# The convolution's output projection by seven products for each two feature tiles, with layer 1's memory values made in layer 0

## The chip, the core and the metric

The kernel runs on one core of a Trainium2 chip. The metric is the device time of one execution in microseconds (us). A core has five engines that work side by side, each through a list of instructions of its own: TensorE (PE; its weight loads are shown apart as PEld), VectorE (DVE), ScalarE (ACT), GpSimd (POOL) and SyncE (SP). In this kernel SP issues all transfers between DRAM and the on-chip memory SBUF. TensorE writes its results into banks of a second memory, PSUM, which VectorE and ScalarE read.

## The reference

A trunk of two layers over 1024 tokens with 1024 features, in float32. Layer 0 is windowed attention beside a retention, layer 1 a gated short convolution, and behind each stands a cross-attention into 256 memory tokens:

```
def conv_mixer(xn, w_in, conv_w, conv_b, w_out):
    gb, gc, u, gate = jnp.split(xn @ w_in, 4, axis=-1)
    z = gc * u
    ...                                 # conv = causal convolution of z over 3 tokens
    y = gb * conv * jax.nn.silu(gate)
    return y @ w_out

def memory_cross_attention(xn, memn, wq, wkv, wo):
    q = xn @ wq
    k, v = jnp.split(memn @ wkv, 2, axis=-1)
    ...
    return softmax(q k^T / 16) v @ wo   # 4 heads of 256

for i in range(2):
    x = x + (even_mixer if i == 0 else conv_mixer)(rmsnorm(x, ...), ...)
    x = x + memory_cross_attention(rmsnorm(x, c_norm[i]), rmsnorm(mem, c_mem_norm[i]), ...)
return rmsnorm(x, final_norm)
```

Rewritten here is `y @ w_out` in layer 1; moved is the half `v` of `memn @ wkv` of layer 1.

## The kernel before

x is kept transposed, as eight tiles of 128 features by 1024 tokens. Each float32 product is made as three products of split halves: a value is its rounded half (hi) plus the rest (lo), and `mm3` (L189, L190, L191) multiplies hi by hi, lo by hi and hi by lo. A split is a cast on ScalarE (L205) and a subtraction on VectorE (L206); for a weight tile L87 and L88, or L106 and L107 where only a page of 512 columns is made. A dense output tile of 128x512 is 8 x 3 = 24 products of 512 columns.

The stages, by their place in the span: layer 0's mixer (0 to about 455 us), its output projection with the memory values of layer 0 (to 545), the cross-attention (to 693), the output projection of that (`out_proj_halves`, to 815: eight output tiles for the first token half, beside which `keys_out` makes layer 1's memory keys and stores them in DRAM, then eight for the second), the convolution's input projection (`conv_in`, to about 1133), its output projection (`out_proj`, to 1240), the second cross-attention (to 1380) and the last projection.

`conv_in` already makes two output tiles at a time by seven products in place of eight, the Strassen-Winograd scheme on 2x2 blocks: `right_factors` makes from the normalized x the blocks B11, B21, B22 and the differences T1 to T4, each of four tiles of 512 columns, split; the class `Weights` makes from two weight tiles the factors A11, A12, A22 and the sums S1 to S4 (S1 to S4 on POOL at L99 to L102, or on VectorE); `strassen` runs the products, each 4 x 3 = 12 of 512 columns, and copies a finished product out of PSUM where a second one needs it (`kept`, L642). `times` multiplies the outputs into z and y (on POOL at L683, for one half of each).

`out_proj` before makes the eight output tiles densely, 16 x 24 = 384 products. For each it loads the old residual tile (`xold`, L287), adds it when the result leaves PSUM (L291), squares the result over `xold` (ACT, L247), adds that to the sum of squares `ssq` (POOL, L249) and stores the new tile (L297). Between them `mem_v` makes the memory values, 96 products, from memory tiles that layer 1 loads again. Behind it `norm` makes R, the reciprocal root of the mean square: two products with a matrix of ones for each token half (L256, L257), then ACT and VectorE (L228 to L233); products of the next stage (q, banks `psd`) run under it and are scaled by R as they leave PSUM (L278).

What sets the order: every tile is one of a few rotating buffers of its tag, so its first write waits for the last reader of the buffer's former tile. The context orders each engine's list by a simulated timeline and gives the listed order; `issue_after` binds one instruction behind another. Weights stream in the order of one list (`order`), two raw tiles at a time (WRAW), three split ones ahead (WHI, WLO). The buffers by tag:

```
BUFS = {"xh": 8, "xl": 8, "r": 8, "e": 4, "T": 5, "v": 4, "t": 5, "k": 4, "n": 2}
```

`v` holds the `xold` tiles; the PSUM banks are three of tag `d`, two `sc` and three `a`.

Of the kernel before, what the change touches and what calls it, by code (L numbers as in the profile page):

```python
# [22 lines left out]
P = 128  # L23
# [8 lines left out]
EARLY = 4  # L32
# [8 lines left out]
class Weights:  # L41
# [5 lines left out]
    FACTORS = ("A11", "A12", "S1", "S2", "S3", "S4", "A22")  # L47
    LATER = FACTORS[2:]

    def __init__(self, tc, pool, sums, order):  # L50
# [10 lines left out]
        for _, f in self.units:  # L61
            self.tags.append(("whi", "wlo") if f is None else (("whi", "wlo")[pages % 2],))
            pages += f is not None
# [4 lines left out]
    def load(self, i):  # L68
# [4 lines left out]
        for k, ap in enumerate(entry[:2] if isinstance(entry, tuple) else (entry,)):  # L73
            t = self.pool.tile([P, D], F32, tag="wraw", bufs=WRAW, name=f"wraw{i}_{k}")
            for c in halves(i == 0):
                self.nc.sync.dma_start(t[:, c], ap[:, c])
# [15 lines left out]
    def factor(self, u, i, f):  # L92
        if f == self.order[i][2][0]:
# [9 lines left out]
            self.factors = F  # L103
        t = self.page(self.tags[u][0], f"wf{u}")
        src, hi, lo = self.factors[f], t[:, :H], t[:, H:]
# [3 lines left out]
        if f == self.order[i][2][-1]:  # L109
            self.raw.pop(i)  # L110

    def prepare(self, upto=None):

        while self.next < len(self.units) and (upto is None or self.next <= upto):
# [6 lines left out]
            if f is None:  # L121
                self.whole(u, i)
            else:
                self.factor(u, i, f)
# [11 lines left out]
class Trunk:  # L136
# [144 lines left out]
    def out_proj(self, ys, x_old, x_new, between=iter(())):  # L281
# [17 lines left out]
        return xs, old  # L299

# [263 lines left out]
    def right_factors(self, x, gain, h, out):  # L564
# [6 lines left out]
             for i in range(2) for j in range(2)}  # L571
        def normed(f):
            for k in range(4):
# [4 lines left out]
        def split(f, src):  # L578
            for k in range(4):
                if f in ("T2", "T1"):  # L580
# [3 lines left out]
                else:  # L584
                    tag = {"B11": "xh", "B21": "xh", "T3": "xl", "B22": "xl", "T4": "Tn"[k // 2]}[f]
                    t = self.buf(tag, f, dt=F32R)
# [12 lines left out]
        T2 = [t[:, i, :] for t in (self.buf("T", "T2", (P, 2, H)) for _ in range(2)) for i in range(2)]  # L599
# [23 lines left out]
        with ExitStack() as behind:  # L623
            for make in (t1, t2, t3, lambda: split("B22", B["B22"]), t4):
                last = make()
                behind.enter_context(self.tc.issue_after(last.ins))
                behind.enter_context(self.tc.issue_after(self.last_cast.ins))

    def strassen(self, B, out, early=False):
# [3 lines left out]
        def product(ps, f, first, weights=None):  # L633
            ah, al = weights or self.w.take()
            with self.tc.issue_after(self.last_mm.ins) if early == 0 and early is not False else ExitStack():
# [4 lines left out]
        def kept(ps):  # L640
            t = self.buf("t", "kept", (P, H))
            self.nc.scalar.copy(t, ps)  # L642
            return t

        a, b = self.ps("sc" if early is False or early < 2 else "d"), self.ps("d")
        if early is False:
            product(a, "B11", True)
            p1 = kept(a)
            product(b, "B21", True)
# [428 lines left out]
```

## Time and profile before

| | us |
|---|---|
| median of 3 runs | 1484.68 (1483.44 to 1486.18) |
| the profiled execution | 1482.23 |
| its span in the profile | 1480.1 |
| span of the rewritten stage, about | 1134 to 1240 |

The span is the time from the first to the last instruction that the profile shows; 2.1 us of the execution lie around it. A page of the profile lists for each engine the busy time, the share of the span and the number of instructions. A row of groups names line, engine, operation, output <- inputs with shapes and the count, then total busy us, mean ns, and what ended the idle time before them. A row of the timeline gives start, length, engine, line and operation, and in brackets the idle time of that engine before it and what ended that. In a table by stretch, the first numbers are the stretch and its length, then busy us (and instructions) of PE, PEld, DVE, ACT and POOL, then TensorE's granted clock as a share of full speed, the DMA engines' busy share and GB/s.

### The profile page before, as it was taken

The numbers are of one execution on the slowest core, as the hardware profiler recorded it, in microseconds if no ns is written. First come the engines' busy times: TensorE is split into PE (matmuls) and PEld (weight loads), VectorE is DVE, ScalarE is ACT, GpSimd is POOL, SyncE is SP. The second block draws the span as 40 slices with busy tenths as digits, with TensorE's granted clock in tenths as the row PEclk, the third lists the DMA queues.
The fourth block names the chain that finished last, engine by engine and source line by source line (L and its number), as shares of the span: only waits on it lengthen the run. The fifth ranks groups of instructions, "written<-read, shape, count | busy, mean of one in ns | idle before, by whom it ended". The sixth has DMA issues, their size and how long they took to land.

```text
span 1480.1 us, 18711 instructions
## 1 busy us (share of the span) xinstructions
PE 1438.2 (97%) x7218; PEld 1215.4 (82%) x7218; DVE 878.1 (59%) x1289; ACT 634.8 (43%) x1139; POOL 322.7 (22%) x201
## 2 busy tenths in 40 slices
PE   8999999999899999999999799999999999999996
PEld 6888888888788888888888578888888888888996
DVE  7656765656674346446456967666665337446555
ACT  6434662334463344335344533333352325335554
POOL 2300103233311110000213455333340220000233
PEclk9999999999999999999999899999999999999999
DMA  6410114221365421013764121111125532111364
GB/s 216 149 65 29 58 30 142 61 79 48 119 224 170 151 92 43 29 42 129 226 201 143 42 86 58 57 57 57 58 86 213 186 128 72 39 33 40 127 210 152
DMA packets 51625, 153.38 MB, mean 104 GB/s; under 512 B 6352, under 2 KB 14672, under 8 KB 51024
## 3 DMA queue, kind: packets, MB, share of 16 engines
q1 hardware_dynamic: 51536, 152.19, 31.7%
q8 instruction: 57, 0.93, 0.3%
q14 instruction: 32, 0.26, 0.1%
HBM read 122.80 MB, written 25.17 MB: 100 GB/s over the span
## 4 chain that ended last, share of the span: by engine, by line
PE 79%; DVE 8%; DMA 5%; POOL 3%; issue 2%; ACT 2%; SPq 0%; DVEq 0%; POOLq 0%; ACTq 0%
PE psd L191 17%; PE psd L189 17%; PE psd L190 17%; PE pssc L191 5%; PE pssc L189 5%; PE pssc L190 5%; PE psa L190 4%; PE psa L189 4%; PE psa L191 4%; DMA swap<-bk 1%; PE pssc L367 1%; DMA swap<-bq 1%; PE psa L397 1%; PE psa L871 1%; POOL bk L432 1%
## 5 line engine op out<-in xcount | busy, mean ns | idle before, releaser
L189 PE MATMUL psd<-xh,whi 128*128 128x512 f32 (+2 forms) x1096 | 414.2, 381 | 7.7 <-ACT whi L87 7.3
L190 PE MATMUL psd<-xl,whi 128*128 128x512 f32 (+2 forms) x1096 | 414.7, 379 | 0.0
L191 PE MATMUL psd<-xh,wlo 128*128 128x512 f32 (+2 forms) x1096 | 414.3, 379 | 0.2 <-DVE wlo L88 0.2
L189 PEld LDWEIGHTS psd<-xh,whi 128*128 128x128 f32 x1096 | 206.4, 188 | 43.2 <-ACT whi L87 7.8
L191 PEld LDWEIGHTS psd<-xh,wlo 128*128 128x128 f32 x1096 | 206.3, 188 | 35.6 <-DVE wlo L88 0.7
L190 PEld LDWEIGHTS psd<-xl,whi 128*128 128x128 f32 x1096 | 206.5, 188 | 34.0
L87 ACT CAST whi<-wraw 128x1024 fp32r<-128x1024 f32 (+1 forms) x135 | 140.8, 1045 | 213.9 <-PE psd L190 131.0
L88 DVE TENSOR_TENSOR wlo<-wraw,whi 128x1024 fp32r<-128x1024 f32 (+1 forms) x135 | 169.1, 1254 | 71.1 <-ACT whi L87 71.0
L249 POOL TENSOR_TENSOR ssq<-ssq,xold 128x512 f32<-128x512 f32 (+2 forms) x54 | 84.6, 1567 | 574.5 <-ACT xold L247 503.0
L106 ACT CAST wf<-ws 128x512 fp32r<-128x512 f32 x64 | 39.7, 622 | 95.2 <-PE pssc L191 27.7
L291 DVE TENSOR_TENSOR xnew<-psd,xold 128x512 f32<-128x512 f32 x32 | 21.9, 690 | 96.4 <-PE psd L191 93.1
L189 PE MATMUL pssc<-T,wf 128*128 128x512 f32 x168 | 67.1, 399 | 6.6 <-ACT T L205 4.2
L190 PE MATMUL pssc<-T,wf 128*128 128x512 f32 x168 | 67.2, 400 | 1.9 <-DVE T L206 1.9
L191 PE MATMUL pssc<-T,wf 128*128 128x512 f32 x168 | 66.9, 398 | 0.0
L247 ACT ACTIVATE xold<-xnew 128x512 f32<-128x512 f32 (+2 forms) x63 | 36.5, 580 | 66.9 <-DVE xnew L291 37.1
L107 DVE TENSOR_TENSOR wf<-ws,wf 128x512 fp32r<-128x512 f32 x64 | 51.8, 811 | 20.7 <-ACT wf L106 19.6
L107 DVE TENSOR_TENSOR wf<-wraw,wf 128x512 fp32r<-128x512 f32 x40 | 55.1, 1393 | 5.0 <-ACT wf L106 5.0
L205 ACT CAST Th<-psa 128x512 fp32r<-128x512 f32 (+1 forms) x62 | 34.3, 588 | 54.2 <-PE psa L871 29.5
L206 DVE TENSOR_TENSOR Tl<-psa,Th 128x512 fp32r<-128x512 f32 (+1 forms) x62 | 41.7, 686 | 21.4 <-ACT Th L205 21.1
L278 DVE TENSOR_TENSOR q<-psd,R 128x512 f32<-128x512 f32 x32 | 22.1, 691 | 53.8 <-PE psd L191 53.8
L99 POOL TENSOR_TENSOR ws<-wraw 128x512 f32<-128x512 f32 x15 | 32.0, 2131 | 90.5 <-DMA wraw<-w_o_in 90.5
L189 PE MATMUL psd<-y,whi 128*128 128x512 f32 x128 | 50.0, 391 | 0.0
(324 smaller groups left out, 2949.4 us busy)
## 6 DMA issues: line engine op xcount, KB each, us to landing
wraw<-w_o SPq DMA_DIRECT2D x40, 512.0 KB, 4.2
wraw<-w_o_in SPq DMA_DIRECT2D x36, 512.0 KB, 3.6
wraw<-w_e_in SPq DMA_DIRECT2D x25, 512.0 KB, 3.6
wraw<-w_k SPq DMA_DIRECT2D x16, 512.0 KB, 3.9
xold<-x SPq DMA_DIRECT2D x16, 512.0 KB, 5.1
wraw<-w_v SPq DMA_DIRECT2D x16, 512.0 KB, 3.8
x<-xnew SPq DMA_DIRECT2D x16, 512.0 KB, 2.6
wraw<-w_q SPq DMA_DIRECT2D x16, 512.0 KB, 3.5
```

The lines of the kernel that those rows point to most:

```text
L87: self.nc.scalar.copy(hi[:, c], raw[:, c])
L88: self.nc.vector.tensor_tensor(lo[:, c], raw[:, c], hi[:, c].bitcast(F32), op=ALU.subtract)
L99: tt(F["S1"], F["A21"], F["A22"], op=ALU.add)
L106: self.nc.scalar.copy(hi, src)
L107: self.nc.vector.tensor_tensor(lo, src, hi.bitcast(F32), op=ALU.subtract)
L189: mm(o, ah, bh, start=first, stop=False, skip_group_check=more)
L190: mm(o, ah, bl, start=False, stop=False, skip_group_check=more)
L191: self.last_mm = mm(o, al, bh, start=False, stop=last, skip_group_check=more)
L205: self.last_cast = self.nc.scalar.copy(hi, src)
L206: return (eng or self.nc.vector).tensor_tensor(lo, src, hi.bitcast(F32), op=ALU.subtract)
L247: nc.scalar.activation(sq, x, AF.Square)
L249: eng.tensor_tensor(self.ssq[:, a:b], self.ssq[:, a:b], sq, op=ALU.add)
```

## The change

In words:

- `out_proj` of layer 1 becomes `out_proj_pairs`: four pairs of output tiles by seven products of 12, so 4 x 84 = 336 products instead of 384. The right factors are made from y (`right_factors` with no gain): B11 and T1 split into buffers of `xh`, T3 and B22 of `xl`, B21 and T2 of `e`, T4 two tiles of `T` and two of `v`; the four tiles of T2 before its split use two more of `v`.
- The residual: a pair's two `xold` tiles are loaded (L323) when the pair first keeps a product; the keep itself adds the residual (VectorE, L330, in place of a copy on ScalarE). When a result leaves PSUM the kept tile is added (L341, L343), the result is squared over `xold` and summed on POOL (L257).
- `OUT_EARLY = 2`: the B11 product of pairs 0 and 1 is run ahead, with its weights (512 columns) paged on their own; its keep is a copy, and the residual is added later.
- The memory values of layer 1 are made beside the keys in layer 0 (`values_out`), split, stored in DRAM and loaded again by `values_in`. The weights `w_v1` move there in the list; the second load of the memory tiles is gone.
- In `conv_in` the product of T4 comes before that of B22 (the factors' order changes with it), B22 is split last, and the multiplication of a half output by `second` goes from POOL to VectorE (L763).

The core of the diff:

```diff
-EARLY = 4
+EARLY, OUT_EARLY = 4, 2
...
+    def out_proj_pairs(self, B, x_old, x_new, early):
+        nc = self.nc
+        half = (slice(0, H), slice(H, S))
+        xs, rest, seen = [None] * KT, {}, set()
+        def pair(n):
+            old, new = [], []
+            def fetch():
+                for i in range(2):
+                    old.append(self.buf("v", "xold"))
+                    nc.sync.dma_start(old[i], x_old[2 * n + i])
+                new.extend(self.buf("r", "xnew") for _ in range(2))
+                xs[2 * n : 2 * n + 2] = new
+            def keep(i, j, ps):
+                t = self.buf("t", "kept", (P, H))
+                if i == j == 0 and n < early:
+                    nc.scalar.copy(t, ps)
+                    return t
+                if not old:
+                    fetch()
+                nc.vector.tensor_tensor(t, ps, old[i][:, half[j]], op=ALU.add)
+                return t
+            def out(i, j, ps, more):
+                c = half[j]
+                x, sq = new[i][:, c], old[i][:, c]
+                if i == j == 0 and n < early:
+                    nc.vector.tensor_tensor(sq, sq, more, op=ALU.add)
+                    more = None
+                nc.vector.tensor_tensor(x, ps, sq if more is None else more, op=ALU.add)
+                end = 2 * n + 2 == KT and i != j
+                self.squares(j in seen, x, sq, c.start, c.stop, None if end else nc.gpsimd)
+                seen.add(j)
+                if end:
+                    rest[j] = sq
+                nc.sync.dma_start(x_new[2 * n + i][:, c], x)
+            return self.strassen(B, out, keep, None, n < early)
...
-            for make in (t1, t2, t3, lambda: split("B22", B["B22"]), t4):
+            for make in (t1, t2, t3, t4, lambda: split("B22", B["B22"])):
...
         product(a, "T2", False)
-        u2 = kept(a)
+        u2 = keep(0, 1, a)
         product(a, "T3", False)
         out(1, 1, a, p5)
+        product(a, "T4", False)
+        out(1, 0, a, None)
         product(c, "B22", False)
         out(0, 1, c, u2)
-        product(a, "T4", False)
-        out(1, 0, a, None)
...
-                    nc.gpsimd.tensor_tensor(c, c, kept[0], op=ALU.mult)
+                    nc.vector.tensor_tensor(c, c, kept[0], op=ALU.mult)
...
-        self.out_proj_halves(ys, xd[0], xd[1], self.keys_out(self.mem_parts(1, "T")), after)
+        mem = self.mem_parts(1, "T")
+        both = (None for _ in zip(self.keys_out(mem), self.values_out(mem)))
+        self.out_proj_halves(ys, xd[0], xd[1], both, after)
         ys = self.conv_in(B)
         self.new_norm()
-        mem = self.mem_parts(1, "T")
-        K = self.keys_in()
-        kv = self.mem_v(mem)
-        V = next(kv)
-        ys = [self.split_k(y) for y in ys]
-        x, rest = self.out_proj(ys, xd[1], xd[2], kv)
+        B = {}
+        for h in range(2):
+            self.right_factors(ys, None, h, B)
+        x, rest = self.out_proj_pairs(B, xd[1], xd[2], OUT_EARLY)
+        K, V = self.keys_in(), self.values_in()
```

Where the lists change. Names are those of the program with a running number; `wraw` is a raw weight tile, `ws` a weight sum, `psd`, `pssc` and `psa` PSUM tiles, `x2` behind a row two of the same. POOL's list before, in the output projection, one row a residual tile:

```order
L249 TENSOR_TENSOR ssq_1058_9171<-ssq_1058_9171,xold_1089_9320 128x512 x2
L249 TENSOR_TENSOR ssq_1058_9171<-ssq_1058_9171,xold_1093_9426 128x512 x2
L249 TENSOR_TENSOR ssq_1058_9171<-ssq_1058_9171,xold_1099_9530 128x512 x2
L249 TENSOR_TENSOR ssq_1058_9171<-ssq_1058_9171,xold_1103_9636 128x512 x2
L249 TENSOR_TENSOR ssq_1058_9171<-ssq_1058_9171,xold_1107_9702 128x512 x2
L249 TENSOR_TENSOR ssq_1058_9171<-ssq_1058_9171,xold_1111_9768 128x512 x2
```

POOL's list now, from the middle of the stage on (9642 and 9644 are the residual tiles of pair 1, 9767 and 9769 of pair 2, 9913 and 9915 of pair 3):

```order
L102 TENSOR_TENSOR ws_1132_9797<-wraw115_1_9780 128x512
L104 TENSOR_TENSOR ws_1132_9797<-wraw115_0_9778,wraw115_1_9780 128x512
L257 TENSOR_TENSOR ssq_1072_9359<-ssq_1072_9359,xold_1115_9642 128x512
L103 TENSOR_TENSOR ws_1133_9798<-ws_1132_9797,wraw115_0_9778 128x512
L257 TENSOR_TENSOR ssq_1072_9359<-ssq_1072_9359,xold_1116_9644 128x512
L105 TENSOR_TENSOR ws_1133_9798<-wraw115_0_9778,ws_1133_9798 128x512
L257 TENSOR_TENSOR ssq_1072_9359<-ssq_1072_9359,xold_1125_9767 128x512
L257 TENSOR_TENSOR ssq_1072_9359<-ssq_1072_9359,xold_1126_9769 128x512
L257 TENSOR_TENSOR ssq_1072_9359<-ssq_1072_9359,xold_1125_9767 128x512
L257 TENSOR_TENSOR ssq_1072_9359<-ssq_1072_9359,xold_1126_9769 128x512
L257 TENSOR_TENSOR ssq_1072_9359<-ssq_1072_9359,xold_1137_9913 128x512
L257 TENSOR_TENSOR ssq_1072_9359<-ssq_1072_9359,xold_1138_9915 128x512
```

Between the sums of squares stand the sums for the weight factors, and each residual tile comes back twice with other work between.

SP's list before, as the third and the fourth residual tile are issued:

```order
L287 DMA xold_1093_9426<-x1_2_200 128x1024
L76 DMA wraw107_0_9305<-w_v1 128x1024
L287 DMA xold_1099_9530<-x1_3_201 128x1024
L76 DMA wraw108_0_9327<-w_o_out 128x1024
L297 DMA x2_0_206<-xnew_1084_9220 128x1024
L287 DMA xold_1103_9636<-x1_4_202 128x1024
```

SP's list now, from pair 2's residual tiles (9767, 9769) to those of pair 3 (9913, 9915):

```order
L323 DMA xold_1125_9767<-x1_4_202 128x1024
L323 DMA xold_1126_9769<-x1_5_203 128x1024
L79 DMA wraw116_0_9924<-w_q1 128x1024
L349 DMA x2_4_210<-xnew_1127_9771 128x512
L912 DMA K_1145_10029<-kd_6023 128x2048
L912 DMA K_1146_10030<-kd_6023 128x2048
L349 DMA x2_4_210<-xnew_1127_9771 128x512
L79 DMA wraw117_0_9961<-w_q1 128x1024
L349 DMA x2_5_211<-xnew_1128_9772 128x512
L323 DMA xold_1137_9913<-x1_6_204 128x1024
L349 DMA x2_5_211<-xnew_1128_9772 128x512
L79 DMA wraw118_0_9997<-w_q1 128x1024
L323 DMA xold_1138_9915<-x1_7_205 128x1024
```

Pair 3's loads stand behind stores of pair 2's results and between loads of the next stage's weights and of the keys.

TensorE's list at the border of pairs 2 and 3 now, from the end of pair 2's T4 (pssc 9750) to the start of pair 3's T2 (pssc 9896); before, dense tiles followed each other without a product that waits for a residual:

```order
L197 MATMUL pssc_1123_9750<-T4_1094_9443,wf217_9751 128x512
L198 MATMUL pssc_1123_9750<-T4_1094_9443,wf217_9751 128x512
L199 MATMUL pssc_1123_9750<-T4_1094_9443,wf217_9751 128x512
L197 MATMUL psd_1175_10107<-xh_1149_10037,whi226_9957 128x512
L197 MATMUL psd_1176_10133<-xh_1149_10037,whi226_9957 128x512
L197 MATMUL pssc_1135_9896<-T2_1085_9404,wf222_9858 128x512
```

Two products of the next stage (`psd` from `xh`) stand between, and T2 adds onto a bank whose former content must have been kept.

TensorE's list at the norm before, around the second product of the first token half (L257):

```order
L191 MATMUL psd_1145_9968<-xh_1127_9914,wlo206_9772 128x512
L189 MATMUL psd_1145_9968<-xh_1129_9918,whi206_9771 128x512
L257 MATMUL psa_1136_9932<-sq2_1135_9931,mean_dr_77 128x512
L190 MATMUL psd_1146_9994<-xl_1128_9915,whi206_9771 128x512
L191 MATMUL psd_1146_9994<-xh_1127_9914,wlo206_9772 128x512
L189 MATMUL psd_1146_9994<-xh_1129_9918,whi206_9771 128x512
L191 MATMUL psd_1147_10026<-xh_1125_9910,wlo207_9838 128x512
```

and at the norm now (psa 10071 and 10086 are the two token halves):

```order
L264 MATMUL psa_1166_10071<-sq2_1165_10070,mean_dr_77 128x512
L264 MATMUL psa_1170_10086<-sq2_1169_10085,mean_dr_77 128x512
L198 MATMUL psd_1175_10107<-xl_1164_10066,whi226_9957 128x512
L199 MATMUL psd_1175_10107<-xh_1163_10065,wlo226_9958 128x512
L198 MATMUL psd_1176_10133<-xl_1164_10066,whi226_9957 128x512
L199 MATMUL psd_1176_10133<-xh_1163_10065,wlo226_9958 128x512
L198 MATMUL psd_1177_10165<-xl_1164_10066,whi227_9993 128x512
L199 MATMUL psd_1177_10165<-xh_1163_10065,wlo227_9994 128x512
L265 MATMUL psa_1166_10071<-sq2_1165_10070,mean_dr_77 128x512
L265 MATMUL psa_1170_10086<-sq2_1169_10085,mean_dr_77 128x512
L197 MATMUL psd_1178_10191<-xh_1149_10037,whi227_9993 128x512
```

The two halves' statistics have moved together, with six q products between their first and their second product, and the fourth tile of q (psd 10191), for which one of the three `d` banks must come free, follows directly; before, that tile came 35 rows behind the first half's last product.

More of the change, by code (lines that the diff above doesn't have):

```diff
@@ L60, in __init__ @@
         pages = 0
-        for _, f in self.units:
-            self.tags.append(("whi", "wlo") if f is None else (("whi", "wlo")[pages % 2],))
-            pages += f is not None
+        for i, f in self.units:
+            paged = f is not None or order[i].shape[-1] < D
+            self.tags.append((("whi", "wlo")[pages % 2],) if paged else ("whi", "wlo"))
+            pages += paged
         self.next = 0
@@ L74, in load @@
             t = self.pool.tile([P, D], F32, tag="wraw", bufs=WRAW, name=f"wraw{i}_{k}")
[L75 removed]
+            t = t[:, : ap.shape[-1]]
+            for c in halves(True) if i == 0 else (slice(0, ap.shape[-1]),):
                 self.nc.sync.dma_start(t[:, c], ap[:, c])
@@ L103, in factor, with paged @@
             self.factors = F
+        self.paged(u, self.factors[f])
+        if f == self.order[i][2][-1]:
+            self.raw.pop(i)
+    def paged(self, u, src):
         t = self.page(self.tags[u][0], f"wf{u}")
-        src, hi, lo = self.factors[f], t[:, :H], t[:, H:]
+        hi, lo = t[:, :H], t[:, H:]
         self.nc.scalar.copy(hi, src)
@@ L120, in prepare @@
             self.load(i)
-            if f is None:
+            if f is None and len(self.tags[u]) == 1:
+                self.paged(u, self.raw.pop(i)[0])
+            elif f is None:
                 self.whole(u, i)
@@ L299, in out_proj @@
         return xs, old
+    def out_proj_pairs(self, B, x_old, x_new, early):
[33 more added lines that the diff above has]
+            return self.strassen(B, out, keep, None, n < early)
+        started = []
+        for n in range(early):
+            started.append(pair(n))
+            next(started[n])
+        for n in range(KT // 2):
+            for _ in started[n] if n < early else pair(n):
+                pass
+        return xs, rest
     def out_proj_halves(self, ys, x_old, x_new, between, after):
@@ L638, in product @@
                     self.mm3(ps, ah[:, c], al[:, c], bh, bl, first and k == 0, k == 3, not first)
[L640 to L646, printed above, removed]
+        a = self.ps("sc" if early is None or early < 2 else "d")
+        if early is None:
             product(a, "B11", True)
-            p1 = kept(a)
-            product(b, "B21", True)
+            p1 = keep(0, 0, a)
+            if apart:
+                yield
         else:
@@ L674, in times, with keep @@
         kept = []
+        def keep(i, j, ps):
+            t = self.buf("t", "kept", (P, H))
+            nc.scalar.copy(t, ps)
+            return t
         def out(i, j, ps, more):
@@ L689, in out @@
                 nc.vector.tensor_tensor(c, ps, c, op=ALU.mult)
-        return self.strassen(B, out, early)
+        return self.strassen(B, out, keep, early)
     def conv_start(self, B):
```

87 lines of the change are left out of this document (64 added, 23 removed).

## The prediction

> **What bounds the kernel now.** I read the page first, then a table by stage, then the waits of TensorE, then the timeline at the places that the change touches.
>
> ```profile
> span 1480.1 us, 18711 instructions
> PE 1438.2 (97%) x7218; PEld 1215.4 (82%) x7218; DVE 878.1 (59%) x1289; ACT 634.8 (43%) x1139; POOL 322.7 (22%) x201
> ```
>
> TensorE is busy for 97% of the span, so a product that goes saves its whole time, and a wait put in costs its whole length. The table by stage has, for each stretch, its length, the busy time of PE, PEld, DVE, ACT and POOL, the granted clock, the DMA share and GB/s. First the first half of layer 0's out projection, then the start of the convolution, then the stage that is rewritten:
>
> ```profile
> 705.00:764.00 59.00, 59.00 (x339) 52.10 (x338) 26.66 (x33) 21.91 (x31) 10.25 (x6) 1.00 0.74 231
> 815.00:860.00 45.00, 36.02 (x135) 27.12 (x133) 39.88 (x61) 22.09 (x38) 21.88 (x7) 0.89 0.17 54
> 1134.00:1240.00 106.00, 105.77 (x467) 87.11 (x466) 47.42 (x51) 40.17 (x48) 18.46 (x12) 1.00 0.43 149
> ```
>
> The rewritten stage has no slack to win: 0.23 us idle in 106. The place in this kernel where a stage of seven products starts already, 815 to 860, has 9.0 us of idle time and a clock of 0.89. The waits of TensorE say the same, for 1130 to 1300 and then (the largest two) for 680 to 900:
>
> ```profile
> PE psd L191 <- DVE wlo L88: 0.2, 1, 0.2
> ...
> PE pssc L189 <- ACT T L205: 4.2, 1, 4.2
> PE pssc L189 <- ACT kept L642: 2.4, 1, 2.4
> ```
>
> The question is thus whether 336 products can be fed as densely as the 384 were. One product's time, and the chain behind a finished tile:
>
> ```profile
> 1179.18 0.39 PE L189 MATMUL psd<-xh,whi 128*128 128x512 f32 x1
> ...
> 1183.71 0.39 PE L191 MATMUL psd<-xh,wlo 128*128 128x512 f32 x1
> ...
> 1184.14 0.69 DVE L291 TENSOR_TENSOR xnew<-psd,xold 128x512 f32<-128x512 f32 x1 [4.30 <-PE psd L191]
> ...
> 1184.91 0.62 ACT L247 ACTIVATE xold<-xnew 128x512 f32<-128x512 f32 x1
> ...
> 1185.68 1.74 POOL L249 TENSOR_TENSOR ssq<-ssq,xold 128x512 f32<-128x512 f32 x1 [3.76 <-ACT xold L247]
> ...
> 1187.44 0.33 SPq L287 DMA_DIRECT2D xold<-x  x1
> ```
>
> From the first to the second row are 20 starts in 4.53 us: 0.2265 us each. The last product of a tile starts at 1183.71; the residual is added, squared (over the old residual tile) and summed on POOL from 1185.68, 1.97 us after that product. Right at the end of the sum (1187.42) SP issues the next residual load: the load waited for the slot.
>
> **The change, part by part.**
>
> *48 products fewer:* 48 x 0.2265 = 10.9 us gained. The 96 value products only move to layer 0.
>
> *Convolution start.* The copy of the kept product stood behind four casts on ACT:
>
> ```profile
> 837.79 0.62 PE L191 MATMUL pssc<-T,wf 128*128 128x512 f32 x1
> 838.08 2.17 ACT L205 CAST B<-xnew 128x512 fp32r<-128x512 f32 x4
> ...
> 840.16 0.57 ACT L642 COPY kept<-pssc 128x512 f32<-128x512 f32 x1
> 840.78 0.50 PE L189 MATMUL pssc<-T,wf 128*128 128x512 f32 x1 [2.38 <-ACT kept L642]
> ```
>
> With B22's split last the copy follows the product's end (837.79 + 0.62) at once: about 1.5 us gained. T4 before B22 in the later pairs only reorders the same products. The multiplication of y and `second` goes from POOL to VectorE, which is 59% busy; next to the end of the stage it shortens the chain. Taken together 0 to 2, counted at 1.5.
>
> *The residual tiles.* The two T4 tiles hold two of the four `v` slots throughout the new stage, so a pair's residual tiles can be loaded only when the pair before has squared and summed its own in the same slots; before, four tiles rotated and a load ran about three tiles ahead. Now the load has a consumer at once: keeping a product adds the residual, and T2 and B22 wait for it. The prices: the POOL sum, the landing of the load in this stretch and, in the next line, over all its issues:
>
> ```profile
> L249 POOL TENSOR_TENSOR ssq<-ssq,xold 128x512 f32<-128x512 f32 x12 | 18.5, 1538 | 78.9 <-ACT xold L247 43.4 <-issue 30.7 <-DMA x<-xnew 4.8
> ...
> DMA to landing us min/median/max: 4.3/4.5/4.5
> DMA to landing us min/median/max: 3.1/5.1/6.8
> ```
>
> Pair 3: its first tile takes the slot of pair 2's first. From the last T3 product of pair 2 it is 1.97 to POOL, then the sums of T3 and B22 in a row (2 x 1.54), 4.4 landing and 0.8 for VectorE's add: 10.3 us. Meanwhile TensorE has T4's 12 products, two q products and one more, 15, 3.4 us, and then T2 of pair 3: 6.9 idle. Pair 2: on POOL two sums of the factors of weights S1 and S2 stand between the sums of pair 1 (the last row below has 1.38 us for one): from T3's last product of pair 1 1.97 + 1.54 + 1.38 + 1.38 + 1.54 + 4.4 + 0.8 = 13.0 us against about 39 products, 8.85: 4.15 idle. Pair 1, which is begun early, needs 1.97 + 1.54 + 4.4 + 0.8 = 8.7 against 35 products, 7.9: 0.85. T4 following T3 on the same bank: 0.5 once. Sum 12.4 us. Its ends: with landings of 3.1 and no S sums ahead on POOL about 8, with 6.8 and 1.74 per sum about 17. On SP the weight loads of later pairs stand behind the waiting residual loads; they have a pair's time, and I price them at nothing.
>
> ```profile
> L101 POOL TENSOR_TENSOR ws<-wraw,wraw 128x512 f32<-128x512 f32 x15 | 20.8, 1384 | 0.0
> ```
>
> *The norm behind it.* Before, the statistics' last product is followed by many q products; now q needs the buffers of T3 and B22, which come free with pair 3, so only six q products stand between the two halves' statistics, and the next q product needs a bank that only R can empty. R's chain:
>
> ```profile
> 1242.19 0.39 PE L257 MATMUL psa<-sq,mean_dr 128*128 128x512 f32 x1
> ...
> 1242.62 0.69 ACT L228 ACTIVATE rs<-psa,eps 128x512 f32<-128x512 f32 x1 [0.44 <-PE psa L257]
> ...
> 1244.01 0.63 ACT L230 ACTIVATE rt<-rs 128x512 f32<-128x512 f32 x1
> ...
> 1244.67 0.69 DVE L231 SCALAR_TENSOR_TENSOR rt<-psa,rt 128x512 f32<-128x512 f32 x1 [1.35 <-ACT rt L230]
> ...
> 1245.86 0.69 DVE L233 TENSOR_TENSOR R<-rt,rs 128x512 f32<-128x512 f32 x1
> ...
> 1248.28 0.69 DVE L278 TENSOR_TENSOR q<-psd,R 128x512 f32<-128x512 f32 x1 [1.73 <-PE psd L191]
> ```
>
> R is there 4.36 us after the product; emptying the bank takes 0.69, and between stands a step of the second half's chain, about another 0.7: 5.8 in all, less two products, 0.45: 5.35 idle. Lower end 3 (the halves do not interleave), upper 6.5.
>
> *The clock after a wait.* The row of 4.18 us idle at the convolution's start, and what follows it:
>
> ```profile
> 831.00 0.50 PE L189 MATMUL pssc<-T,wf 128*128 128x512 f32 x1 [4.18 <-ACT T L205]
> ...
> 834.38 0.63 PE L189 MATMUL pssc<-T,wf 128*128 128x512 f32 x1
> ...
> 835.00:838.00 3.00, 3.00 (x9) 2.11 (x7) 3.00 (x6) 2.25 (x4) 3.00 (x1) 0.50 0.00 0
> ```
>
> From 834.38 to 837.79 eight steps take 0.426 us each, at a granted clock of 0.50: about ten slow steps, 2 us, behind one long wait. Two of the new waits are longer than 4.18 (pair 3 and the norm), pair 2's is near: 3.5, from 2 to 7. The Trainium skill, "TensorE: Matmul & The Clock Gate", Part 1, The HAM clock gate, says that about one window (3.4 us) of idling halves the rate until about as long a busy stretch has passed. This trace agrees (0.50, 0.426 against 0.2265); by an estimate from that page alone each long wait would lose 1.7 us.
>
> *The way into the stage.* Before, a y tile's whole split was hidden. Now 28 half splits on ACT and VectorE and 16 subtractions on VectorE stand there, with the weights' sums on POOL, and T2, T3 and T4 need the last y tile. No row shows it for this stage. The low end is the stage as it was (nothing), the high end the convolution's own start, 9.0 us of idle and slow time beyond it, 12. The work is the same as there, but without gains and with the B11 and T1 products of pairs 0 and 1 as cover: 6, nearer to the second.
>
> *Layer 0.* The value products stand beside the keys. In 705 to 764 seven residual loads are issued, so a tile of the first half takes 59 / 7 = 8.4 us. The rows of that stretch's loads, and the cast and the subtraction of a weight tile:
>
> ```profile
> wraw<-w_o SPq DMA_DIRECT2D x10, 512.0 KB, 4.7
> ...
> xold<-x SPq DMA_DIRECT2D x7, 256.0 KB, 3.8
> ...
> L87 ACT CAST whi<-wraw 128x1024 fp32r<-128x1024 f32 (+1 forms) x135 | 140.8, 1045 | 213.9 <-PE psd L190 131.0
> L88 DVE TENSOR_TENSOR wlo<-wraw,whi 128x1024 fp32r<-128x1024 f32 (+1 forms) x135 | 169.1, 1254 | 71.1 <-ACT whi L87 71.0
> ```
>
> With 12 value products it takes 8.4 + 2.7 = 11.1 us and moves 2.62 MB (three weight tiles, keys, values, residual in and out), 235 GB/s; the row at 705 shows 231 GB/s without a wait. Three raw weight tiles go through two slots: 4.7 landing, 1.05 cast, 1.25 subtraction and 0.33 issue are 7.3, so 3.65 us a tile where 3.7 are to be had. That just fits; I take 2, from 0 to 10. Layer 1's stage loses the second load of the memory (four of 512 KB) and gains two loads of the values of 1 MB, off the path.
>
> Sum: -10.9 - 1.5 + 12.4 + 5.35 + 3.5 + 6 + 2 = +16.9 us. The profiled execution took 1482.23 us (span 1480.1), 0.17% under the median of 1484.68 (1483.44 to 1486.18). On the one base that gives 1499.1, on the other 1501.6; I say 1500.
>
> **The rivals.**
>
> *The residual arrives in time.* If a pair's load is issued before the wait counts (some 5.2 us ahead: 4.4 landing and 0.8), the 12.4 us and with them most of the clock loss fall away; norm 5.35 and a way in of 3 to 6 stay: 1484.68 - 12.4 + 5.35 + 3.5 = 1481, from 1476 to 1486. For it: POOL is only 22% busy, and before the load ran ahead. Against it: the slots, which only the sums release. It decides on the other side.
>
> *POOL shut out by VectorE.* A sum of two weight halves at the convolution's start:
>
> ```profile
> 834.20 13.49 POOL L99 TENSOR_TENSOR ws<-wraw 128x512 f32<-128x512 f32 x1 [34.67 <-DMA wraw<-w_o_in]
> ...
> 846.47 0.68 DVE L686 TENSOR_TENSOR second<-pssc,kept 128x512 f32<-128x512 f32 x1
> ```
>
> It took 13.49 us and ended just after VectorE, which had run operations with two SBUF inputs back to back, came to one that reads PSUM. The L101 row's 1.38 is what such a sum takes alone, so a shut-out costs 12.1. The new way in has 44 such VectorE operations (28 + 16) of some 0.6 us and needs POOL's S1 for T1 and S2 for T2; with the 36 products of B11 and T1 as cover (8.2 us), one shut-out leaves 4, two leave 16. This would put the way in at about 14 instead of 6: 1508, from 1503 to 1514. The Trainium skill, "SBUF — State Buffer", Who interferes with whom, states that such a VectorE instruction and a GpSimd one exclude each other for the whole instruction; this trace agrees in the 13.49 us, and what it would make of the time is this rival.
>
> *Layer 0 bound by its transfers.* If landings there grow from 4.7 to 5.5, a raw tile needs 4.05 us instead of 3.7, 24 tiles, 8.4 us: with 2 of it counted already, 1506. For it: 3.65 against 3.7; against it: three pages of split weights lie ahead.
>
> **How the numbers follow.** About 0.2%, 3 us, is what a measurement of this kernel can tell from no change. My forecast, 1500 (1491 to 1505, the ends of the smaller terms), has a chance of 0.50. The residual in time 0.23: 0.16 of it faster by over 0.2%, 0.07 within. POOL shut out 0.18, layer 0 bound 0.09, both slower. Slower 0.77, same 0.07, faster 0.16. The range 1481 to 1511 leaves out half of the first rival and the ends of the others.
>
> **What would show it.** In the profile after: TensorE with some 48 products fewer and a busy share that falls below 97%; waits of the T2 and B22 products of pairs 2 and 3 on the kept products, which sit behind the residual load on VectorE; POOL sums right ahead of SP's residual issues; a wait of about 5 us of the q product on R, with the granted clock under 0.9 behind both; idle time between 1100 and 1150. I am wrong if the kept products of pairs 2 and 3 wait for nothing, or if a q product fills the norm. Then the 10.9 us show in full. If layer 0 is the matter, waits on the split weights stand between 700 and 790.

## The result and the profile after

The changed kernel takes 1506.20 us (median of 4, 1505.49 to 1507.78) against 1484.47 for the kernel before: 1.0147 times as long, 95% interval 1.0129 to 1.0164. (1484.47 is the median of four runs; that of the three named ahead is 1484.68.) The profiled execution took 1505.49 us, its span 1503.4. The page, span and first section:

```profile
span 1503.4 us, 18770 instructions
...
PE 1440.5 (96%) x7170; PEld 1212.1 (81%) x7170; DVE 911.9 (61%) x1373; ACT 652.8 (43%) x1181; POOL 309.4 (21%) x201
```

TensorE has its 48 instructions fewer (7218 to 7170), but is busy for 2.3 us more, and the span has grown by 23.3. Fewer products with more busy time are slower products. The table by stretch (as before: length, then busy us of PE, PEld, DVE, ACT and POOL, the granted clock, the DMA share, GB/s) shows where: layer 0's first half, the way into the stage (two rows), the pairs, and the norm.

```profile
705.00:795.00 90.00, 90.00 (x483) 78.04 (x482) 45.84 (x54) 38.39 (x52) 9.90 (x6) 1.00 0.76 234
...
1120.00:1150.00 30.00, 27.05 (x118) 21.72 (x117) 29.96 (x46) 17.44 (x32) 2.89 (x3) 1.00 0.18 54
1150.00:1182.00 32.00, 26.10 (x94) 19.97 (x95) 29.93 (x35) 14.26 (x23) 11.82 (x7) 0.84 0.31 95
1182.00:1240.00 58.00, 49.70 (x206) 38.67 (x205) 26.98 (x37) 24.61 (x36) 26.16 (x19) 0.97 0.59 199
1240.00:1280.00 40.00, 34.86 (x153) 28.70 (x152) 26.87 (x33) 15.25 (x21) 1.55 (x1) 0.95 0.31 110
```

Layer 0 is full at 234 GB/s: there the values cost their products and nothing else. VectorE is what is full on the way in (29.96 of 30 us, 29.93 of 32). The waits of TensorE from 1120 to 1300, where the kernel before had one of 0.2:

```profile
PE psd L197 <- DVE q L286: 5.1, 1, 5.1
PE psa L197 <- ACT wf L114: 4.9, 3, 2.3
PE pssc L197 <- DVE kept L334: 4.7, 1, 4.7
PE psa L199 <- DVE wf L115: 3.4, 1, 3.4
PE pssc L197 <- DVE xnew L343: 1.6, 2, 0.8
PE pssc L197 <- ACT kept L753: 1.2, 1, 1.2
PE pssc L197 <- ACT wf L114: 0.9, 1, 0.9
PE psa L197 <- DVE kept L334: 0.4, 1, 0.4
```

For a ledger that has the slow products too, I took from TensorE's timeline the time from each start to the next and subtracted 0.2265 us a product (0.12 at 256 columns). What is left is lost time, idle or slow:

| lost us at | before | after | of it idle |
|---|---|---|---|
| convolution's start (815 to 870; 838 to 894) | 15.8 | 15.3 | 8.8 |
| way into the stage | 0.5 | 15.2 | 9.6 |
| borders of the pairs | 0 | 10.7 | 7.5 |
| norm and what follows it | 0 | 7.0 | 5.1 |

32.9 - 0.5 - 0.5 - 10.9 (the products) is 21.0 of the span's 23.3. The rest, 1.8 to 2.3, lies ahead of 455 us, behind a wait on layer 0's keys at 433; that place varies from trace to trace (3.1 to 6.8 us lost from 425 to 470), and none of the kernels differs there in its code. The profiled execution of the kernel before was also 2.2 us under its own median.

The way in, row by row (VectorE, SP, POOL, ACT, TensorE):

```profile
1143.30 0.68 DVE L115 TENSOR_TENSOR wf<-wraw,wf 128x512 fp32r<-128x512 f32 x1
...
1144.02 0.33 SPq L79 DMA_DIRECT2D wraw<-w_o_out  x1
...
1147.71 2.22 POOL L102 TENSOR_TENSOR ws<-wraw 128x512 f32<-128x512 f32 x1 [27.11 <-DVE T L214]
...
1149.96 0.62 ACT L114 CAST wf<-ws 128x512 fp32r<-128x512 f32 x1 [1.05 <-POOL ws L102]
...
1150.63 0.50 PE L197 MATMUL psa<-T,wf 128*128 128x512 f32 x1 [2.34 <-ACT wf L114]
...
1167.63 3.43 DVE L115 TENSOR_TENSOR wf<-ws,wf 128x512 fp32r<-128x512 f32 x2
...
1171.12 0.79 PE L199 MATMUL psa<-T,wf 128*128 128x512 f32 x1 [3.41 <-DVE wf L115]
```

VectorE's subtraction at 1143.30 is the last reader of a half weight tile; at its end SP loads pair 0's second tile into that slot, by the median of this stretch's weight loads, 3.6 us, it lands at 1147.6, and POOL starts at 1147.71. The row puts POOL's wait down to VectorE's split; by these times it was the load. Pair 1 repeats this 16 us later, and there the last y tile's chain fills VectorE as well: two subtractions of 0.69 take 3.43 while POOL makes its sums.

The border of pairs 2 and 3, from T3's result on:

```profile
1227.46 0.69 DVE L343 TENSOR_TENSOR xnew<-pssc,kept 128x512 f32<-128x512 f32 x1 [1.37 <-PE pssc L199]
...
1228.41 0.63 ACT L255 ACTIVATE xold<-xnew 128x512 f32<-128x512 f32 x1
...
1229.12 2.66 POOL L257 TENSOR_TENSOR ssq<-ssq,xold 128x512 f32<-128x512 f32 x2 [9.19 <-ACT xold L255]
...
1231.81 0.32 SPq L323 DMA_DIRECT2D xold<-x  x1
...
1235.65 0.69 DVE L334 TENSOR_TENSOR kept<-pssc,xold 128x512 f32<-128x512 f32 x1 [2.53 <-DMA xold<-x]
...
1236.40 0.50 PE L197 MATMUL pssc<-T,wf 128*128 128x512 f32 x1 [4.68 <-DVE kept L334]
```

This is the chain of the prediction: two sums, the issue at their end, the landing, the add, T2. And the norm: the statistics' last products, R, the emptied bank, the waiting q product.

```profile
1265.35 0.61 PE L265 MATMUL psa<-sq,mean_dr 128*128 128x512 f32 x2
...
1269.05 0.69 DVE L241 TENSOR_TENSOR R<-rt,rs 128x512 f32<-128x512 f32 x1
...
1270.37 1.28 DVE L286 TENSOR_TENSOR q<-psd,R 128x512 f32<-128x512 f32 x2
...
1271.11 0.80 PE L197 MATMUL psd<-xh,whi 128*128 128x512 f32 x1 [5.14 <-DVE q L286]
```

Behind four of these waits the table has the clock at half:

```profile
1152.00:1154.60 2.60, 2.60 (x7) 2.02 (x7) 2.60 (x4) 1.42 (x3) 2.52 (x2) 0.50 0.00 0
1172.00:1175.00 3.00, 3.00 (x8) 2.32 (x8) 3.00 (x6) 0.62 (x1) 0.00 (x0) 0.50 0.00 0
1237.00:1240.00 3.00, 3.00 (x9) 2.33 (x8) 0.76 (x2) 0.63 (x1) 1.28 (x1) 0.50 0.82 258
1272.00:1274.00 2.00, 2.00 (x6) 1.52 (x6) 2.00 (x4) 0.31 (x1) 0.00 (x0) 0.50 0.00 0
```

### The profile page after: what moved, and what is told of

It reads as the page before. It is cut to its first block, busy times and chain, and to the rows that moved or that the text cites. A ratio compares the mean times of both kernels' runs of the same rounds, so it can differ in the third digit from the quotient of the medians.

```text
span 1503.4 us, 18770 instructions
## 1 busy us (share of the span) xinstructions
PE 1440.5 (96%) x7170; PEld 1212.1 (81%) x7170; DVE 911.9 (61%) x1373; ACT 652.8 (43%) x1181; POOL 309.4 (21%) x201
## 4 chain that ended last, share of the span: by engine, by line
PE 75%; DVE 11%; DMA 6%; POOL 3%; ACT 2%; issue 2%; SPq 0%; DVEq 0%; POOLq 0%; ACTq 0%
PE psd L199 14%; PE psd L197 14%; PE psd L198 14%; PE pssc L199 6%; PE pssc L197 6%; PE pssc L198 6%; PE psa L198 4%; PE psa L197 4%; PE psa L199 4%; DVE T L214 1%; DMA wraw<-w_o 1%; DMA swap<-bk 1%; PE pssc L428 1%; DMA swap<-bq 1%; DVE wf L115 1%
## 5 line engine op out<-in xcount | busy, mean ns | idle before, releaser
L197 PE MATMUL psd<-xh,whi 128*128 128x512 f32 (+2 forms) x968 | 365.9, 381 | 13.4 <-ACT whi L90 7.6
L199 PE MATMUL psd<-xh,wlo 128*128 128x512 f32 (+2 forms) x968 | 365.2, 378 | 0.4 <-DVE wlo L91 0.4
L198 PE MATMUL psd<-xl,whi 128*128 128x512 f32 (+2 forms) x968 | 364.9, 378 | 0.0
L197 PEld LDWEIGHTS psd<-xh,whi 128*128 128x128 f32 x968 | 182.7, 189 | 44.5 <-ACT whi L90 8.2
L91 DVE TENSOR_TENSOR wlo<-wraw,whi 128x1024 fp32r<-128x1024 f32 (+1 forms) x127 | 158.8, 1252 | 89.0 <-ACT whi L90 88.9
L199 PEld LDWEIGHTS psd<-xh,wlo 128*128 128x128 f32 x968 | 182.5, 189 | 30.8 <-DVE wlo L91 0.7
L198 PEld LDWEIGHTS psd<-xl,whi 128*128 128x128 f32 x968 | 182.6, 189 | 29.3 <-DVE xl L226 0.2
L257 POOL TENSOR_TENSOR ssq<-ssq,xold 128x512 f32<-128x512 f32 (+2 forms) x54 | 82.7, 1532 | 557.5 <-ACT xold L255 519.2
L197 PE MATMUL pssc<-T,wf 128*128 128x512 f32 x216 | 88.1, 408 | 14.4 <-DVE kept L334 4.7
L115 DVE TENSOR_TENSOR wf<-ws,wf 128x512 fp32r<-128x512 f32 x80 | 78.5, 998 | 22.3 <-ACT wf L114 21.8
L198 PE MATMUL pssc<-T,wf 128*128 128x512 f32 x216 | 86.9, 403 | 1.7 <-DVE T L214 1.6
L199 PE MATMUL pssc<-T,wf 128*128 128x512 f32 x216 | 86.8, 403 | 0.0
L197 PEld LDWEIGHTS pssc<-T,wf 128*128 128x128 f32 x216 | 42.3, 196 | 27.1 <-DVE kept L334 5.6
L198 PEld LDWEIGHTS pssc<-T,wf 128*128 128x128 f32 x216 | 42.1, 195 | 12.1 <-DVE T L214 3.6
```

Of the source, the lines that this page charges most:

```text
L91: self.nc.vector.tensor_tensor(lo[:, c], raw[:, c], hi[:, c].bitcast(F32), op=ALU.subtract)
L115: self.nc.vector.tensor_tensor(lo, src, hi.bitcast(F32), op=ALU.subtract)
L197: mm(o, ah, bh, start=first, stop=False, skip_group_check=more)
L198: mm(o, ah, bl, start=False, stop=False, skip_group_check=more)
L199: self.last_mm = mm(o, al, bh, start=False, stop=last, skip_group_check=more)
L257: eng.tensor_tensor(self.ssq[:, a:b], self.ssq[:, a:b], sq, op=ALU.add)
```

## The experiments

All times are medians, beside runs of the kernel before on the same chip; the ratio is to those, with its 95% interval.

**One part alone: the values moved (dense_moved).** The kernel before, dense, with this edit and the weights' list to match:

```diff
-        K = self.keys_in()
-        kv = self.mem_v(mem)
-        V = next(kv)
+        K, V = self.keys_in(), self.values_in()
         ys = [self.split_k(y) for y in ys]
-        x, rest = self.out_proj(ys, xd[1], xd[2], kv)
+        x, rest = self.out_proj(ys, xd[1], xd[2])
```

> The kernel before with one part of the change alone: layer 1's values made beside the keys in layer 0; the output projection stays dense, without value products in it. Theory A (the ledger of idle and slow time by stage: layer 0's first half has no wait in the changed kernel, and a dense stage has 63 products of its own, 14 us, in three banks as cover for the last y tile): within 3 us of 1484.5. Rival B (the value products were the cover of the way into the stage, and their move cost it): slower by 5 us or more, with waits around 1150.

Measured 1487.62 against 1485.21, ratio 1.0020 (1.0010 to 1.0029). The time, 2.4 us over its own base, is A's, and B's 5 us are not reached, but the place is B's. Its trace, last y tile, split, waiting product:

```profile
1162.00 1.22 DVE L733 TENSOR_TENSOR cv<-cv,y 128x1024 f32<-128x1024 f32 x1
...
1163.26 1.04 ACT L205 CAST xh<-cv 128x1024 fp32r<-128x1024 f32 x1 [2.62 <-DVE cv L733]
1164.33 1.23 DVE L206 TENSOR_TENSOR xl<-cv,xh 128x1024 fp32r<-128x1024 f32 x1 [1.11 <-ACT xh L205]
1164.35 1.65 PE L189 MATMUL psd<-xh,whi 128*128 128x512 f32 x3 [2.56 <-ACT xh L205]
```

The way in loses 4.2 us in the ledger, where the kernel before loses 0.5. In the dense kernel the value products were the cover of the last y tile: products that do not need that tile and kept TensorE at work while it was made.

**Another part alone: the convolution (conv_only).** The kernel before with the convolution's edits:

```diff
-            for make in (t1, t2, t3, lambda: split("B22", B["B22"]), t4):
+            for make in (t1, t2, t3, t4, lambda: split("B22", B["B22"])):
...
-                    nc.gpsimd.tensor_tensor(c, c, kept[0], op=ALU.mult)
+                    nc.vector.tensor_tensor(c, c, kept[0], op=ALU.mult)
```

> The kernel before with the convolution's part of the change alone (T4's product before B22's, B22 split last, the multiplication of y on VectorE). Theory A (by the ledgers of idle and slow time at the convolution's start, 15.8 us before and 15.3 after): no more than 1 us less, 1483.5 to 1485. Rival B (the prediction's term): 1.5 us less or more, 1483 or below.

Measured 1485.26 against 1485.71, ratio 0.9999 (0.9989 to 1.0009). A's time, and again another place than either: the ledger at the start falls by 1.8 (17.1 to 15.4, from 810 to 900), as the prediction had it, and 2.2 more than before are lost at the convolution's end (2.8 against 0.6, from 1130 to 1150), by two waits that the kernel before does not have:

```profile
PE pssc L189 <- ACT whi L87: 1.3, 1, 1.3
PE pssc L189 <- DVE z L689: 0.8, 1, 0.8
```

Which of the edits makes these two waits was not run apart.

**The residual's slot (own_tiles).** The residual is loaded into the tile of the result and added in place; the squares go into scratch:

```diff
-                    old.append(self.buf("v", "xold"))
-                    nc.sync.dma_start(old[i], x_old[2 * n + i])
+                    nc.sync.dma_start(new[i], x_old[2 * n + i])
...
-                x, sq = new[i][:, c], old[i][:, c]
+                x, sq = new[i][:, c], self.buf("v", "sq", (P, H))
```

> The changed kernel, with each residual tile loaded into the tile of its own result and summed in place, the squares into scratch tiles of 512 columns: a load no longer waits for the sums of the pair before. Theory A (the residual's slot makes the 4.7 us wait on the kept product between pairs 2 and 3, and the slow clock behind it another 1.9): the wait is gone, 6 to 7 us less than 1506, about 1499.5. Rival B (the wait only moves to the squares, the stores or the banks): at most 2 us less, 1504 or more.

Measured 1496.04, ratio 1.0077 (1.0061 to 1.0092): 10 us less than the changed kernel, more than A's 6 to 7. The four pairs' stretch in its table has 0.13 us idle in 58:

```profile
1184.00:1242.00 58.00, 57.87 (x256) 47.61 (x255) 38.49 (x43) 25.80 (x37) 29.22 (x19) 1.00 0.57 204
```

All border losses went with it (0.4 of 10.7 are left in the ledger), the waits on L343 too: with the loads early, the scheduler has other products to put between T3 and T4. The way in (16.0 lost) and the norm (a wait of 5.1) stay.

**The raw weight tiles (half_raw).** The half tiles for the early B11 products get a raw buffer of their own:

```diff
-            t = self.pool.tile([P, D], F32, tag="wraw", bufs=WRAW, name=f"wraw{i}_{k}")
-            t = t[:, : ap.shape[-1]]
+            small = ap.shape[-1] < D
+            t = self.pool.tile([P, ap.shape[-1]], F32, tag="whalf" if small else "wraw",
+                               bufs=1 if small else WRAW, name=f"wraw{i}_{k}")
```

> The changed kernel, with the two half weight tiles for the early B11 products in a raw buffer of their own, so that the two raw slots take pair 0's tiles at once. Theory A (the wait at 1150 is the late load of pair 0's second raw tile, issued at 1144.02 when a half tile left its slot, landed at 1147.7): the load is issued about 8 us earlier, that wait of 2.3 us and the slow clock behind it (4.2 together) go: 1502. Rival B (POOL is shut out by VectorE's operations, the load is no matter): 1506, and the sums start no earlier.

Measured 1506.11 (1502.84 to 1507.09), ratio 1.0139 (1.0122 to 1.0157): no gain that the medians show, so the time is B's, though the sums do start earlier. The load was the matter for that one wait, but not for the way in. POOL now starts some 10 us earlier, and the wait of 2.3 us on S1 is gone; in its place the kept product is late, and VectorE's full list stretches the sum:

```profile
1137.01 5.95 POOL L103 TENSOR_TENSOR ws<-wraw 128x512 f32<-128x512 f32 x1 [18.05 <-DMA wraw<-w_o_out]
...
1140.08 0.50 PE L198 MATMUL pssc<-T,wf 128*128 128x512 f32 x1 [2.52 <-ACT kept L754]
```

In the ledger the way in loses 13.8 instead of 15.2; that trace is of an execution 3.3 us under the median.

**The sums on VectorE (vector_sums).** In the weights' list, for pairs 0 and 1:

```diff
+              + ((True,) if i < 2 * OUT_EARLY else ()) for i in range(0, len(o_out), 2)]
```

> The changed kernel, with the weight sums of pairs 0 and 1 made on VectorE in place of POOL. Theory A (the sums wait for late raw tiles; VectorE is full from 1130 to 1165): no gain, and 8 more operations of 0.69 us in a full queue: 1506 to 1511. Rival B (POOL shut out by VectorE, the rival of the prediction): the waits on S1 and S2 go, 1498 to 1502.

Measured 1503.29, ratio 1.0124 (1.0109 to 1.0139): 3 us less, between the two; in the ledger the way in loses 12.3 instead of 15.2. That is a balance of two things. VectorE's operations on 128x512 start 0.60 us apart where nothing holds them up. In the changed kernel eight of them run beside POOL's sums for pairs 0 and 1 (1149 to 1155 and 1164 to 1171) and take 7.3 us more than that together; one of them:

```profile
1150.40 1.77 DVE L115 TENSOR_TENSOR wf<-wraw,wf 128x512 fp32r<-128x512 f32 x1
```

On VectorE the eight sums themselves add 8 x 0.60 = 4.8 us, and the difference, 2.5, is near what was measured. So POOL's sums cost VectorE's full list about 7 us; that is an estimate from these rows, and no run has the way in without these sums on either engine. With the residual in its own tile as well (own_vec):

> The changed kernel with the residual in its result's tile and the sums of pairs 0 and 1 on VectorE, both. Theory A (the two losses lie in different stretches, borders of pairs and the way in): the gains of 10 and 3 us add up, 1493. Rival B (what is won on the way in is lost again before the first border): 1496.

Measured 1491.34, ratio 1.0040 (1.0027 to 1.0054). The gains add up, A, and about 2 us more.

**The last y tile (no_taps).** own_vec, with the two shifted taps left out for the last of the eight tiles:

```diff
-            nc.vector.scalar_tensor_tensor(cv[:, 1:], z[:, : S - 1], w[1], cv[:, 1:],
+            if m < KT - 1:
+                nc.vector.scalar_tensor_tensor(cv[:, 1:], z[:, : S - 1], w[1], cv[:, 1:],
```

> As own_vec, with the two shifted taps of the convolution left out for the last of the eight tiles: two VectorE operations of 1.28 us fewer in the chain from the last convolution product to the last y tile. Theory A (the last part of the way in, 7.9 us of idle and slow time in own_vec, waits for that chain): 2 to 3.5 us less than own_vec, 1488 to 1489.3. Rival B (it waits for weights): the same as own_vec, 1491.

Measured 1487.09, ratio 1.0019 (1.0009 to 1.0029): A: 3.1 us less by the ratios, 4.2 by the medians. The largest wait of own_vec from 1120 to 1250, a B tile split late, is the first row here; the largest of no_taps is the second:

```profile
PE psd L197 <- ACT B L213: 3.5, 1, 3.5
```

```profile
PE pssc L197 <- ACT kept L753: 1.3, 1, 1.3
```

With two operations of 1.28 us on VectorE the wait on B goes too.

**More cover (own_q4, own_q4_e3, own_q4_e4).** First, own_vec with the fourth q tile in a spare bank:

```diff
-                self.dense(xs, self.scaled(lambda a, b: q[dt][:, a:b]))
+                self.dense(xs, self.scaled(lambda a, b: q[dt][:, a:b]),
+                           tags=("d", "sc") if head == 0 and dt and not paged else "d")
```

> As own_vec, with the fourth q tile of the second cross-attention in a free bank of tag sc, so that its products can run before R is there. Base: own_vec, 1491.3. Theory A (the norm's wait of 5.1 us and the slow clock behind it, 7.8 together, stand because only three q banks are to be had): wait and slow products shrink by 2 to 5 us, 1486.5 to 1489.5. Rival B (R's chain starts as much later as products are put ahead of the statistics): 1491.

Measured 1490.13, ratio 1.0036 (1.0022 to 1.0049): B. The scheduler put most of the fourth tile's products ahead of the statistics, so R came as much later, and the wait stands at 5.2:

```profile
PE psd L197 <- DVE q L286: 5.2, 1, 5.2
```

Then `OUT_EARLY` of 3 and 4, with the banks of the further B11 products from tag d:

```diff
-EARLY, OUT_EARLY = 4, 2
+EARLY, OUT_EARLY = 4, 4
...
-        a = self.ps("sc" if early is None or early < 2 else "d")
+        a = self.ps(bank if early is None else "sc" if early < 2 else "d")
```

> As own_q4, with the B11 product of a third pair run early: 12 products, 2.7 us, more that do not need the last y tile. Theory A (the way into the stage lacks cover, which the value products were in the dense kernel): up to 2.7 us less than own_q4. Rival B (the way in is bound by VectorE's list and the raw weight tiles; one more half tile to load and split makes it longer): the same as own_q4 or up to 2 more.

> As own_q4, with all four B11 products early: 24 products, 5.4 us, more. Theory A (cover): 4 to 5.4 us less than own_q4, near 1483. Rival B (VectorE's list and the raw tiles): the same as own_q4 or up to 4 more.

Measured 1488.36 (ratio 1.0026, 1.0015 to 1.0037) and 1487.46 (1.0017, 1.0006 to 1.0027). With all four early it is 2.7 us less than own_q4, half of the added products' time: the way of A, but not its 4 to 5.4. With three the medians differ by 1.8 us; that is not clear of the scatter, and its trace is only 0.5 us shorter over this stretch. With all four early, own_q4's 3.5 us on B is down to 0.8, and the largest wait on the way in is 1.3:

```profile
PE pssc L197 <- ACT T L213: 1.3, 1, 1.3
...
PE psd L197 <- ACT B L213: 0.8, 1, 0.8
```

**The clock (warm_before, own_warm).** Products into a spare bank that nothing reads, behind a chosen product:

```diff
+    def warm(self, n, tag, ah, bh):
+        ps = self.ps(tag)
+        with self.tc.issue_after(self.last_mm.ins):
+            for _ in range(n):
+                self.nc.tensor.matmul(ps, ah, bh, start=True, stop=True)
```

> The kernel before with 16 products more, 3.6 us, into a spare bank that nothing reads, right behind the last T1 product at the convolution's start, in the 4.2 us that TensorE waits there. Theory A (the idle time itself slows the clock: about 4.7 us of slow products follow these waits): the products behind them run at 0.2265 us and 2 to 4.5 us are gained, 1480 to 1482.5. Rival B (the clock follows something else, as the load of VectorE and POOL in that stretch): no gain, 1484.5 to 1486.

Measured 1485.14 against 1485.71, ratio 0.9999 (0.9990 to 1.0009): no gain, so B by the time. The trace says something else:

```profile
836.70 0.50 PE L189 MATMUL pssc<-T,wf 128*128 128x512 f32 x1 [0.54 <-ACT T L211]
839.06 0.50 PE L190 MATMUL pssc<-T,wf 128*128 128x512 f32 x1 [1.86 <-DVE T L212]
839.40 0.40 PE L191 MATMUL pssc<-T,wf 128*128 128x512 f32 x1
...
843.81 0.50 PE L189 MATMUL pssc<-T,wf 128*128 128x512 f32 x1 [1.92 <-ACT kept L649]
...
846.03 0.63 PE L190 MATMUL pssc<-T,wf 128*128 128x512 f32 x1
```

The products behind the first waits are fast now (starts 0.23 us apart from 839.40 on; 0.426 before), and by 848 this trace has made up 2.7 us on that of the kernel before. But the next products wait for VectorE and ACT, the clock halves behind the wait of 1.92 us (in the kernel before, behind one of 2.38 there), and by 905 only 1.2 us are left, too little for the medians to tell from nothing. The same spare products were tried once more at this place and at two others (own_warm: own_vec with 16 there, 8 behind the second early B11, 18 at the norm):

> As the kernel with both (own tiles, sums on VectorE), with products that nothing reads in three waits: 16 at the convolution's start, 8 behind the second early B11 product, 18 behind the statistics at the norm. Theory A (idle time slows the clock): the slow products behind the norm's wait (1.85 us), on the way in (2 of the 5) and at the convolution's start (2 to 4.5) go, 6 us less than without: 1487. Rival B (the clock follows something else): as without, 1493, or some us more by the products themselves.

Measured 1489.38 against own_vec's 1491.34, ratio 1.0024 (1.0015 to 1.0034): 2 us, not 6. At the norm:

```profile
1249.92 4.24 PE L216 MATMUL pssc<-xh,mean_dr 128*128 128x512 f32 x18
...
1255.23 0.50 PE L197 MATMUL psd<-xh,whi 128*128 128x512 f32 x1 [1.07 <-DVE q L292]
1255.57 0.39 PE L198 MATMUL psd<-xl,whi 128*128 128x512 f32 x1
```

The q products behind are at full rate: 4.1 us for the 18 products and 1.35 lost against 7.8 lost in own_vec. That is 2.35 us, all of what the run gained. At the convolution's start nothing came of it (0.1 us): there the same two waits, 0.54 and 1.86, have seven products at half rate behind them, where warm_before has none:

```profile
856.85 0.79 PE L198 MATMUL pssc<-T,wf 128*128 128x512 f32 x1 [1.86 <-DVE T L220]
```

So it is not shown that the spare products made the fast stretch of warm_before. At the norm they are the likelier cause: in each of the nine traces with a wait of 5.1 to 5.5 us there, slow products follow.

No version of the changed kernel beat the kernel before. The nearest, own_q4_e4, is 0.06 to 0.27% slower; that together with the norm's spare products wasn't tried.

## Why the prediction was right, point by point

Direction and size were right (1500, range 1481 to 1511; 1506.2 measured), at 15.3 us forecast and 21.7 found. But the time lies above the narrower range of the main forecast (1491 to 1505), and inside that of the rival with POOL. Part of the nearness is luck: the way in cost 9.2 us more than its term, while the residual tiles with their share of the clock cost some 3.5 less, layer 0 cost nothing, and about 2 us of the span's difference lie ahead of 455, where the change does not reach. The terms:

- *48 products, -10.9:* the count is as said, and nothing suggests another price.
- *Residual tiles, 12.4, and a share of the clock's 3.5:* 10.7 lost in the ledger, slow products included; removed whole by own_tiles (10 us). The mechanism is shown for pair 3. The split was off: pair 3's wait is 4.7, not 6.9 (a sum took 1.33, not 1.54, and the load 3.8, not 4.4, and TensorE's T4 waited 0.8 first). Pair 2's 4.15 is about 0.2: TensorE's list has the B11 and T1 products of pair 3 there, 24 of them. Pair 1's 0.85 is 0.4, T4 on T3's bank cost 0.8 at two borders, not 0.5 once, and a late weight factor 0.9 more. What the first rival describes, the residual in time, is own_tiles: 1496.0, not 1481, since the way in loses 16.0 there where that sum takes 3 to 6.
- *Norm, 5.35:* 5.14, and 1.85 slow behind it. Shown by the rows of R's chain. Here the working was right.
- *The clock, 3.5:* the two places that it named lost 1.9 each, 3.7. Its pattern was misread: between the wait of 4.18 us and the slow products stands a second one, of 1.86 (831.00 to 833.36), so they do not follow one long wait. And the way in lost 5.6 more by slow products, which no term held. By the Trainium skill's rule ("TensorE: Matmul & The Clock Gate", Part 1: The HAM clock gate), which has about 3.4 us of idling ahead of the half rate, the way in would have lost little, since only the last of its single waits (0.8 to 3.4 us) comes near that. Here seven slow products followed a wait of 2.34 us; the measurement decides.
- *The way into the stage, 6 (nothing to 12):* the term that was mis-sized: 15.2, above its own upper end. One step that failed is "The 96 value products only move": I priced their products, not the cover that they gave to the last y tile. The dense kernel loses 3.7 us there without them. The pairs lose more; what fits that is that T2, T3, T4, B21 and B22 all wait for that tile, that VectorE's list is full, and that the raw tiles are released by that same list. How the 15.2 divide among these is not shown. No single mend removes them: raw buffers 0 to 2 us, sums off POOL 3, less in the last tile's chain 3 to 4, more cover 2.7.
- *POOL shut out, the rival at 0.18:* present, but not as priced. The rival had 12 us lost by one sum on POOL; in the changed kernel none of pairs 0 and 1 took over 2.22, and it is VectorE's full list that was held up, by some 7 us (the estimate at vector_sums). One sum took 5.95 us in half_raw, where it began earlier. Taking the sums off POOL won 3 us, not 8. The Trainium skill's rule that such instructions exclude each other ("SBUF — State Buffer", Who interferes with whom) agrees with 5.95 and with the two subtractions of 3.43 us. By its time alone, 1506.2 in 1503 to 1514, this rival stands as well as the forecast; what speaks against it as the whole cause are the 2.22 and the 3 us.
- *Convolution's start, -1.5:* 1.8 there in conv_only, given back at the convolution's end, 0 in all. The forecast had no term for the end.
- *Layer 0, 2:* nothing at 234 GB/s. The rival that it becomes bound by transfers is refuted.

## What to carry to other kernels

A product that is moved out of a stage takes its cover with it: before pricing the move at nothing, ask which chain it covered, and look in the trace for what ends latest beside it. A scheme with fewer products pays only where its operands are early; here it turned a stage without waits into one with three places of them. Two are buffers that the former holder gave back late (a residual's slot, a PSUM bank); the third is the way in, where VectorE's list is full and a raw tile's slot is one part. Loading an operand into the buffer of the result it belongs to took away one of them whole.

## What the runs showed of the hardware

The clock can halve behind a wait shorter than 4 us, and the length of the wait alone does not tell whether it will. In the fourteen traces, from 800 to 1300 us, TensorE waits 30 times for 2.8 us or more, and each time products at half rate (0.43 us apart) follow within 6 us. Behind waits of 1.0 to 2.6 us they follow in some places and not in others: seven after 2.34 us in the changed kernel, none after 2.52 us in half_raw (the next eleven start 0.23 us apart), and after the same 0.54 and 1.86 us seven in own_warm and none in warm_before. What decides there is not shown. And a VectorE operation with two SBUF inputs is stretched by POOL as POOL is by it: 0.69 us alone, 1.15 to 1.77 beside POOL's sums.
